# Operand tiles moved to multiples of 512 bytes in a gMLP and SSD trunk

## The chip, the cores and the metric

The kernel runs on one core of one Trainium2 chip. The metric is device time in microseconds of one execution; the time before is 1432.25 us, the median of three runs (1432.12 to 1435.49). The engines are TensorE (PE in the profile; its weight loads are PEld), VectorE (DVE), ScalarE (ACT), GpSimd (POOL) and SyncE (SP), which issues the loads. ScalarE's queue issues the stores.

## The reference

One layer on a sequence of 1024 positions with D = 1024. A normalised and modulated input h is projected to 11,296 columns, which feed two branches: a chunked spatial gating unit (gMLP) and a chunked state-space scan (SSD, 32 heads of 64, 8 groups). Both are projected back, gated, added, projected by w_out and added to the input; a last normalisation follows.

```python
mod = jax.nn.silu(c) @ ada_w + ada_b
shift, scale, gate = jnp.split(mod, 3, axis=-1)
h = rms_norm(x, norm_w) * (1 + scale[:, None, :]) + shift[:, None, :]
proj = h @ w_in
gm_u, gm_v, gm_z, ssm_z, xbc, dt_raw, g_a, g_b = jnp.split(proj, SPLITS, axis=-1)
y_a = spatial_gating(gelu(gm_u), gelu(gm_v), ...) * silu(gm_z)
xbc = silu(causal_depthwise_conv(xbc, conv_w, conv_b))
xs, bm, cm = jnp.split(xbc, ...)
dt = softplus(dt_raw + dt_bias)
a = -jnp.exp(a_log)
y_b = ssd_scan(xs as heads, dt, a, bm, cm) + xs * d_skip[:, None]
y_b = rms_norm(y_b * silu(ssm_z) by group)
merged = sigmoid(g_a) * (y_a @ w_proj_a) + sigmoid(g_b) * (y_b @ w_proj_b)
out = rms_norm(x + gate[:, None, :] * (merged @ w_out), final_norm_w)
```

## The kernel before

Nearly all matmuls of the projections work on float32r operands of 128 rows, with a stationary tile of 128 columns and a moving tile of 512. Each float32 operand is split into a high part (rounded to float32r) and the rest, and a product of two operands is three matmuls per block of 128: high with high, high with low, low with high. The small products of the state-space part are plain float32.

The work runs in five stages.

- The first stage (pool `p0`, to about 74 us) loads x and the modulation weights, computes h transposed, and writes it as the moving operands `bop` (names b11, t1, t2, b22, t3, b21, t4, each high and low, four tiles of 128 × 512). They stay in the pool `hp`, and after the products are done the same slots hold other operands. `first_products` makes the first 256 columns and dt beside it.
- The products (L563, `product`; to about 926 us) go over 43 pairs of 128-column blocks of w_in. A pair is done in a Winograd-like form with seven products of twelve matmuls. The weights of the pair after next are loaded to `wsp` (names a and s) and split into `wp` (names p..h and p..l). Each product ends with `run_tasks`, which runs small jobs that `later` put down for a number of products ahead: dt, the mixing weights, the gate, w_proj_b. The results go to the wide tiles `w4` and from there to DRAM.
- The state-space stage (to about 1176 us) runs chunks for eight groups (`Group`), with the projection by w_proj_a (`pma`) filled in between.
- The merge by w_proj_b (L1437, `multiply`; to about 1336 us) has 56 units of twelve matmuls. Its stationary tiles (p1a to p4a) lie in the pools `p2r` and `p2q`, its moving tiles (bh, bl) in `hp`.
- The output product (`out_product`, tiles po) multiplies merged rows (stationary mh and ml in `hp`, mmh and mml in `p2r` and `p2q`) with gated w_out (moving, woh and wol in `hp`).

Memory is laid out by pools. On the left a pool begins where the one opened before it ends: four small constants that the framework puts behind a scratch area of 16 KB, then `const`, `hp`, and then by turns `p0`, `wp` and `wsp`. On the right pools grow down from the top: `w4`, then `gm` and `gx` (later `prepool`), and after the products `p2r`, `p2x` and `p2q`. Within a pool tiles lie one behind the other, padded to 32 bytes. A pool that is opened with `reuse_waits="tile"` makes each of its tiles wait for the earlier tiles that it overlaps. The `const` pool holds 7,936 bytes per partition, among them `dtb`, `abc` and `dsk` of 128 bytes each (L112, L113, L115). At the narrowest, when `p2q` is open, left and right are 96 bytes apart (139,136 and 139,232).

The three small constants are used so: `dsk` is loaded in the first stage (L437) and two copies take it to `dskt` in `small_parameters` (L417). `dtb` and `abc` are loaded at the same place (L435, L436) and read in `dt_part1a` (L653) and `dt_part1d` (L680 to L682), some 670 us later.

The builder's planner sets the order of what isn't pinned (`pin` keeps program order) by its own estimate of times; TensorE's matmuls and the loads are pinned.

Of the kernel before, what the change touches and what calls it, by code (L numbers as in the profile page):

```python
# [8 lines left out]
F32 = mybir.dt.float32  # L9
# [7 lines left out]
P = 128  # L17
# [6 lines left out]
NH = 32  # L24
# [11 lines left out]
def hybrid_kernel(  # L36
# [33 lines left out]
    def cst(shape, name, dt=F32):  # L70
        return const.tile(shape, dt, name=name, tag=name)
# [9 lines left out]
    def f32(t):  # L81
        return t.bitcast(F32)

    def load(dst, src):
        pin(nc.sync.dma_start(dst, src))
# [23 lines left out]
    par = cst([P, P], "par")  # L109
    par2 = cst([P, P], "par2")  # L110
    cwt = cst([P, P], "cwt")
    dtb = cst([P, NH], "dtb")  # L112
    abc = cst([P, NH], "abc")  # L113
    dskt = cst([P, 16], "dskt")
    dsk = cst([P, NH], "dsk")  # L115
    sc = cst([P, KT], "sc")
    dthq = cst([P, NCH * NH], "dthq")
    dde = cst([P, NCH * NH], "dde")
# [30 lines left out]
    def last_split(nm):  # L149
# [2 lines left out]
        pin(A.copy(hi, t))  # L152
        pin(V.tensor_sub(lo, t, f32(hi)))

    w4pool = tc.tile_pool(name="w4pool", bufs=1, side="right", reuse_waits="tile")
    w4p = w4pool.__enter__()
    w4 = [w4p, 6]

    def wide(name, dt=F32):
        return w4[0].tile([P, S], dt, name=name, tag="w4", bufs=w4[1])  # L160


    with tc.tile_pool(name="p0", bufs=1, reuse_waits="tile") as p0:
# [8 lines left out]
        def aw_tile(n):  # L172
            return p0.tile([P, KT, 2, P], F32, name=f"aw{n}", tag="aw", bufs=2)

        hf2 = {}

        def hf_tile(k, h):
# [18 lines left out]
        def load_aw(n):  # L196
            k = KS[n]
            if n:
                aw[n] = aw_tile(n)
            for j in range(2):  # L200
                load(aw[n][:, :, j, :],
                     ada_w[:, j * D + k * P : j * D + (k + 1) * P].rearrange("(k p) c -> p k c", p=P))

        def load_w0(n):
            k = KS[n]
            raw = p0.tile([P, W0], F32, name=f"w0r{n}", tag="w0r", bufs=2)
            wd = p0.tile([P, 2 * NH], F32R, name=f"w0d{n}", tag="w0d", bufs=2)
            hi, lo = (p0.tile([P, 256], F32R, name=f"w0{v}{n}", tag=f"w0{v}", bufs=2) for v in "hl")
            load(raw, w_in[k * P : (k + 1) * P, COL_DT : COL_DT + W0])
            wk[n] = (raw, wd, hi, lo)  # L210

        def split_w0(n):
            raw, wd, hi, lo = wk[n]
            pin(A.copy(hi, raw[:, NH:W0]))
            pin(A.copy(wd[:, 0:NH], raw[:, 0:NH]))
            pin(V.tensor_sub(lo, raw[:, NH:W0], f32(hi)))
            pin(V.tensor_sub(wd[:, NH:], raw[:, 0:NH], f32(wd[:, 0:NH])))
# [119 lines left out]
        def first_products(n):  # L337
            raw, wd, wh, wl = wk[n]
            for h in halves(n):
                hh, hl = hhs[n, h]  # L340
                for m, (lw, r) in enumerate(((wh, hh), (wl, hh), (wh, hl))):
                    for i in (1, 2):
                        mm(accs[i][h], lw[:, i * P - P : i * P], r, n + m == 0, n == KT - 1 and m == 2)
                        yield
                for nd, r in ((2 * NH, hh), (NH, hl))[:: 1 if n == 0 else -1]:
                    mm(accs[0][h][0:nd, :], wd[:, 0:nd], r, n == 0 and r is hh, n == KT - 1 and r is hh)
                    yield
# [46 lines left out]
        def prepare(n):  # L394

            if n == 1:
                return {
                    8: lambda: (warm(6), transposes(0, 1), rows_of_h(0, 1), matvec(1), warm(5)),
                    11: lambda: (transposes(1, 1), modulation(1), rows_of_h(1, 1)),
                    16: lambda: (transposes(1, 0), rows_of_h(1, 0)),  # L400
                }
            a, b = halves(n)
            return {
                2: lambda: (matvec(n), transposes(n, a)),
                6: lambda: (modulation(n), rows_of_h(n, a)),
                14: lambda: (transposes(n, b), rows_of_h(n, b)),
            }

        def small_parameters():
            pp = ax("pp1")  # L410
            for i in range(2):
                tp(pp[:, i * P : (i + 1) * P], pkb[:, i], ident)
            for i in range(2):
                pin(V.tensor_copy((par2, cwt)[i], pp[:, i * P : (i + 1) * P]))
            for hh in range(2):
                part = slice(hh * HD, (hh + 1) * HD)
                pin(V.tensor_copy(dskt[part, :], dsk.rearrange("p (i h) -> p i h", h=2)[part, :, hh]))  # L417
# [10 lines left out]
        for n in range(KT):  # L428
            todo = prepare(n + 1) if n + 1 < KT else {}
            for at, _ in enumerate(first_products(n), 1):  # L430
                if at == 1 and n + 2 < KT:
                    load_aw(n + 2)
                    load_w0(n + 2)
                if at == 1 and n == 1:
                    load(dtb, dt_bias.to_broadcast([P, NH]))  # L435
                    load(abc, a_log.to_broadcast([P, NH]))  # L436
                    load(dsk, d_skip.to_broadcast([P, NH]))  # L437
                if at in todo:
                    todo[at]()
                for f, kk in sums.get((n, at), ()):  # L440
                    f(kk)
                if at == 2 and 0 < n < KT - 1:
                    split_w0(n + 1)
                if n == 4 and at == 8:
                    small_parameters()
# [7 lines left out]
    gm = gmpool.__enter__()  # L453
# [27 lines left out]
    def later(delay, f, *a):  # L481
        tasks.append((slot[0] + delay, f, a))
# [143 lines left out]


    bsb = gm.tile([P, D], F32, name="bsb", tag="bsb")
    first_c1 = {"v0": gx.tile([P, S], F32, name="c1v0", tag="wst")}
    wst = None  # L630
    bst = gx.tile([P, NCH, NG, 6], F32, name="bst", tag="bst")
# [3 lines left out]
    def dt_part1():  # L635

        dtt = wide("dtt2")[0 : 2 * NH, :]
        load(dtt, dt_d)
        V.tensor_add(fold[0], ident[:, 0:NH], ident[:, NH : 2 * NH])
        sm1 = wide("sm1").rearrange("p (a n) -> p a n", a=4)  # L640
        sm2 = wide("sm2").rearrange("p (a n) -> p a n", a=4)
        later(2, dt_part1a, dtt, sm1, sm2)
# [476 lines left out]
    def stats():  # L1119
        v_stats()  # L1120
        mix_load(0)

    later(216, dt_part1)
    later(9, mix_weights)
    for i in range(4):
# [554 lines left out]
```

## Time and profile before

| | before |
|---|---|
| median of three runs | 1432.25 us |
| profiled execution, span | 1432.7 us |
| PE busy | 1396.2 us, 97% |
| PEld busy | 1152.6 us, 80% |
| VectorE busy | 1024.9 us, 72% |
| ScalarE busy | 785.1 us, 55% |
| GpSimd busy | 205.7 us, 14% |
| mean clock of TensorE | 0.997 |
| DMA moved | 277.08 MB, 193 GB/s |

The profile is one execution. A matmul's duration there (some 390 ns) is modelled and overlaps with the next one's, so busy TensorE isn't TensorE at its best. How fast matmuls follow each other is read from their starts: in the timeline, or in the chain of waits, where a merged row "2.72 PE zx L563 x12" stands for twelve matmuls, one behind the other. The trace lacks some matmul records, so counts are taken from the code where they matter. An instruction's shape stands behind its name (128*128 128x512: array rows and columns used, then the moving tile).

### The profile page before, as it was taken

To read this page: it belongs to the slowest core of one execution; us is meant where nothing else is said; L and a number is where in the kernel's file an instruction comes from. 1 tells how busy PE (TensorE), PEld (TensorE's weight loads), DVE (VectorE), ACT (ScalarE), POOL (GpSimd) and SP (SyncE) were. 2 spreads that over 40 slices of the span, in tenths; PEclk is the share of its full clock that TensorE was granted. 3 is DMA by queue.
4 is the path that set the end of the run, shared out by engine and by line. 5 is a ranking of instruction groups with operands and counts; after the bars stand their busy time and mean duration, and the time that the engine had idled before them with its cause. 6 is when DMAs were issued, how large, how long until landed. Compare 5 with 4: busy or idle time off the path is not lost.

```text
span 1432.7 us, 20518 instructions
## 1 busy us (share of the span) xinstructions
PE 1396.2 (97%) x7087; PEld 1152.6 (80%) x7087; DVE 1024.9 (72%) x1821; ACT 785.1 (55%) x1444; POOL 205.7 (14%) x190
## 2 busy tenths in 40 slices
PE   8999999999999999999999999999989989999997
PEld 6688888888888888888887888877878877787886
DVE  5686776777667888788887784587677767948443
ACT  6664576566656565555665555776667524325101
POOL 0000000000000000000000100057878830000000
PEclk9999999999999999999999999999999999999999
DMA  8552343333332777687677764788778668977332
GB/s 266 162 162 89 118 118 103 107 100 118 103 114 86 205 223 225 190 246 215 195 231 216 220 180 142 268 297 307 254 262 295 215 211 286 352 254 284 124 118 74
DMA packets 260524, 277.08 MB, mean 193 GB/s; under 512 B 13596, under 2 KB 210628, under 8 KB 260420
## 3 DMA queue, kind: packets, MB, share of 16 engines
q1 hardware_dynamic: 179396, 195.37, 43.8%
q10 hardware_dynamic: 81024, 80.40, 16.6%
q8 instruction: 56, 0.92, 0.3%
q14 instruction: 48, 0.39, 0.1%
HBM read 191.40 MB, written 84.31 MB: 192 GB/s over the span
## 4 chain that ended last, share of the span: by engine, by line
PE 78%; DMA 8%; DVE 5%; issue 3%; ACT 3%; POOL 2%; SPq 1%; ACTq 0%; POOLq 0%; DVEq 0%
PE xuz L563 6%; PE po L76 6%; PE xcb L563 6%; PE xx L563 5%; PE xz L563 5%; PE x L1437 5%; PE xg L563 5%; PE pma L76 3%; PE yp L1437 3%; PE yuz L563 3%; PE xv L563 3%; PE ycb L563 3%; PE yx L563 3%; PE yz L563 2%; PE yg L563 2%
## 5 line engine op out<-in xcount | busy, mean ns | idle before, releaser
L770 POOL TENSOR_TENSOR wog<-wog,gb 128x1024 f32<-128x1024 f32 x8 | 21.8, 2722 | 724.8 <-PE xz L563 529.1
L969 ACT ACTIVATE dcy<-dcy,nacs 128x128 f32<-128x128 f32 x256 | 78.5, 389 | 14.4 <-POOL dcy L964 14.2
L964 POOL TENSOR_SCALAR_AFFINE_SELECT dcy<-dcy 128x1024 f32<-128x1024 f32 x32 | 35.1, 1097 | 107.8 <-ACT ea L961 104.1
L961 ACT ACTIVATE ea<-dcy 64x512 f32<-64x512 f32 x64 | 40.1, 627 | 12.6 <-DMA dcy<-acs_d 12.2
L882 ACT ACTIVATE ac<-ac 128x1024 f32<-128x1024 f32 x32 | 34.0, 1061 | 20.0 <-DVE ac L880 19.8
L1643 ACT ACTIVATE xr<-r 128x1024 f32<-128x1024 f32 x7 | 7.4, 1061 | 67.2 <-issue 39.7
L76 PE MATMUL pma<-yh,wah 128*128 128x512 f32 x128 | 43.9, 424 | 0.0
L76 PE MATMUL pma<-yh,wal 128*128 128x512 f32 x128 | 43.2, 419 | 0.0
L1049 DVE TENSOR_TENSOR ym<-yn,ea 128x512 f32<-128x512 f32 (+1 forms) x32 | 19.9, 623 | 31.3 <-PE yn L76 31.2
L1051 POOL TENSOR_TENSOR yz<-y,sl 128x512 f32<-128x512 f32 x32 | 41.9, 1309 | 1.1
L989 DVE TENSOR_TENSOR dcy<-dcy,pc 128x1024 f32<-128x1024 f32 x32 | 39.0, 1217 | 4.3 <-PE pc L79 3.0
L76 PE MATMUL pma<-yl,wah 128*128 128x512 f32 x128 | 40.5, 398 | 0.0
L76 PEld LDWEIGHTS yn<-sl,st 128*128 128x128 f32 x224 | 30.3, 190 | 10.9 <-POOL yz L1051 2.9
L1050 POOL TENSOR_TENSOR y<-y,ym 128x512 f32<-128x512 f32 (+1 forms) x32 | 36.5, 1142 | 16.3 <-DVE ym L1049 16.3
L1633 POOL TENSOR_TENSOR r<-r,fnw 128x256 f32<-128x256 f32 (+1 forms) x3 | 2.7, 916 | 250.7 <-ACT xr L1632 250.7
L76 PE MATMUL yn<-sl,st 128*128 128x128 f32 x224 | 31.7, 276 | 7.1 <-DVE st L1019 7.1
L880 DVE SCALAR_TENSOR_TENSOR ac<-c2x,cwt,ac 128x1023 f32<-128x1023 f32 (+2 forms) x24 | 31.8, 1325 | 9.0 <-ACT ac L878 7.1
L1642 DVE TENSOR_TENSOR r<-po,xr 128x1024 f32<-128x1024 f32 x7 | 8.6, 1225 | 41.1 <-PE po L76 41.1
L76 PE MATMUL sp<-xe,bn 128*128 128x256 f32 x112 | 33.0, 411 | 4.5 <-DVE ym L1049 1.4
L76 PE MATMUL yi<-dcy,xd 128*64 128x128 f32 x512 | 35.9, 284 | 0.0
L880 DVE SCALAR_TENSOR_TENSOR ac<-c2cb,cwt,ac 128x1023 f32<-128x1023 f32 (+2 forms) x24 | 30.6, 1275 | 7.1 <-ACT ac L878 7.0
L1017 POOL TENSOR_TENSOR st<-st,cd 128x256 f32<-128x256 f32 x48 | 32.3, 673 | 10.3 <-PE yn L76 7.2
(2827 smaller groups left out, 4395.4 us busy)
## 6 DMA issues: line engine op xcount, KB each, us to landing
sl<-s_d SPq DMA_DIRECT2D x32, 768.0 KB
s_d<-ac ACTq DMA_DIRECT2D x32, 512.0 KB
dcy<-acs_d SPq DMA_DIRECT2D x32, 512.0 KB
aw<-in_ada_w_dram SPq DMA_DIRECT2D x16, 512.0 KB
wbr<-in_w_proj_b_dram SPq DMA_DIRECT2D x64, 128.0 KB
wb_d<-wbb ACTq DMA_DIRECT2D x32, 256.0 KB
wb_d<-wbc ACTq DMA_DIRECT2D x32, 256.0 KB
yb_d<-yz ACTq DMA_DIRECT2D x32, 256.0 KB
```

Source lines behind the costliest of these rows:

```text
L76: pin(PE.matmul(acc, l, r, start=first, stop=last))
L563: pin(PE.matmul(ps, lw[:, k * P : (k + 1) * P], r[k], start=first and n + k == 0, stop=n == 2 and k == 3, skip_group_check=not first))
L880: V.scalar_tensor_tensor(ac[:, s:], cc[:, : S - s], conv_wt[:, 3 - s, i : i + 1], ac[:, s:], op0=ALU.mult, op1=ALU.add)
L882: A.activation(ac, ac, AF.Silu)
L961: A.activation(ea[hh * HD : (hh + 1) * HD], dcy.rearrange("p (j e) i l -> p e j (i l)", e=2)[hh * HD : (hh + 1) * HD, hh], AF.Exp)
L964: G.affine_select(out=d8, in_=d8, compare_op=ALU.is_ge, fill=-1e30, base=0, pattern=[[0, 2 * HPG], [1, P]], channel_multiplier=-1)
L969: A.activation(dcy[:, h, i, :], dcy[:, h, i, :], AF.Exp, bias=sub[:, i, h : h + 1])
L989: V.tensor_tensor(d3, d3, pc[:, 0:256].unsqueeze(1).to_broadcast([P, HPG, 256]), op=ALU.mult)
L1017: G.tensor_mul(v3(s2), v3(self.st), fac(cd, g, s)[:, i].unsqueeze(2).to_broadcast([P, HPG, HD]))
L1050: G.tensor_add(y1[:, :, t0:], y1[:, :, t0:], m[:, :, t0:])
L1051: G.tensor_mul(yz, y1, sl[:, 4:6])
L1437: pin(PE.matmul(ps[j], a[:, v, js], r, start=first and n + k == 0, stop=n == 2 and k == KT - 1, skip_group_check=not first))
```

## The change

Three things are done to the layout. `dtb`, `abc` and `dsk` leave the pool `const`; `dsk` becomes a tile of `p0`, and `dtb` and `abc` become the first and second 32 columns of a tile `dta` in `gm`. Their loads: `dsk`'s stays; those of the other two move to `dt_part1`, behind the reload of dt. And a pool `edge` with one tile of 120 floats (480 bytes) that nothing uses is opened first on the right.

The left pools behind `const` so move down by 384 bytes, from 24,448 to 24,064 = 47 × 512, and the top of the right pools by 480, from 229,344 to 228,864 = 447 × 512. The left and the right pools then meet at 138,752 when `p2q` is open. The tiles of `p0` behind x lie 128 bytes further along than a multiple would have them, as `dsk` stands before them. No instruction of TensorE, VectorE, ScalarE or GpSimd is added or removed.

```diff
-    dtb = cst([P, NH], "dtb")
-    abc = cst([P, NH], "abc")
     dskt = cst([P, 16], "dskt")
-    dsk = cst([P, NH], "dsk")
...
+    edge = ctx.enter_context(tc.tile_pool(name="edge", bufs=1, side="right"))
+    edge.tile([P, 120], F32, name="edge", tag="edge")
     w4pool = tc.tile_pool(name="w4pool", bufs=1, side="right", reuse_waits="tile")
...
+        dsk = p0.tile([P, NH], F32, name="dsk", tag="dsk")
...
                 if at == 1 and n == 1:
-                    load(dtb, dt_bias.to_broadcast([P, NH]))
-                    load(abc, a_log.to_broadcast([P, NH]))
                     load(dsk, d_skip.to_broadcast([P, NH]))
...
     bsb = gm.tile([P, D], F32, name="bsb", tag="bsb")
+    dta = gm.tile([P, P], F32, name="dta", tag="dta")
+    dtb, abc = dta[:, 0:NH], dta[:, NH : 2 * NH]
...
         load(dtt, dt_d)
+        load(dtb, dt_bias.to_broadcast([P, NH]))
+        load(abc, a_log.to_broadcast([P, NH]))
```

## The prediction

> **What bounds the kernel now.** I read the page first (busy times, clock, chain), then the stages in the view of stretches, then the chain in order of time, and then single matmuls in the timeline of TensorE.
>
> ```profile
> span 1432.7 us, 20518 instructions
> PE 1396.2 (97%) x7087; PEld 1152.6 (80%) x7087; DVE 1024.9 (72%) x1821; ACT 785.1 (55%) x1444; POOL 205.7 (14%) x190
> PEclk9999999999999999999999999999999999999999
> PE 78%; DMA 8%; DVE 5%; issue 3%; ACT 3%; POOL 2%; SPq 1%; ACTq 0%; POOLq 0%; DVEq 0%
> ```
>
> ```profile
> 0.00:74.00 74.00, 66.29 (x470) 49.35 (x471) 42.72 (x106) 48.24 (x90) 3.13 (x10) 1.00 0.70 207
> 74.00:616.00 542.00, 541.63 (x2486) 449.98 (x2485) 413.22 (x687) 327.39 (x521) 1.40 (x1) 1.00 0.47 140
> 616.00:926.00 310.00, 308.79 (x1369) 253.44 (x1368) 230.16 (x413) 178.87 (x310) 23.97 (x10) 1.00 0.68 207
> 926.00:1176.00 250.00, 231.83 (x1686) 200.16 (x1685) 182.96 (x328) 158.23 (x400) 174.41 (x166) 0.99 0.78 267
> 1176.00:1336.00 160.00, 158.86 (x678) 126.66 (x677) 117.71 (x189) 58.53 (x100) 0.00 (x0) 1.00 0.81 281
> 1336.00:1422.00 86.00, 86.00 (x386) 70.42 (x385) 34.58 (x90) 12.09 (x22) 1.28 (x1) 1.00 0.30 104
> ```
>
> In the second fence the columns are stretch, length, busy time (instructions) of PE, PEld, DVE, ACT and POOL, clock, DMA share, GB/s. TensorE is busy nearly everywhere, at full clock, and carries 78% of the chain. So what counts is how long one matmul takes, not whether TensorE waits. The chain gives that: almost pure TensorE from 78 to 616 us, products of 12 matmuls in 2.72 us.
>
> ```profile
> 212.28 2.72 PE zx L563 x12
> ...
> 853.21 3.02 PE xx L563 x12
> ```
>
> That is 226.7 ns for each matmul of 512 columns. Later products take up to 3.02 us, and DMAs and VectorE enter the chain there. Is 226.7 ns the array's own time? This stretch of the state-space stage has the clock at 0.50 (eighth number), and two matmuls stand there in 0.85 us:
>
> ```profile
> 1170.60:1173.28 2.68, 2.68 (x7) 2.11 (x8) 2.52 (x5) 1.76 (x3) 2.10 (x1) 0.50 0.93 316
> ...
> 1171.58 1.05 PE L76 MATMUL pma<-yl,wah 128*128 128x512 f32 x2
> 1172.43 1.05 PE L76 MATMUL pma<-yh,wal 128*128 128x512 f32 x2
> ```
>
> So 512 columns take 425 ns at half clock, 212.5 ns if all of it scaled to full clock. The product's matmul pays 14 ns more at full clock, for something that does not get faster with the array. A plain float32 matmul of 256 columns, which passes each column twice and so asks for its moving operand at half the rate, does not pay it:
>
> ```profile
> 933.25 0.81 PE L76 MATMUL sp<-xe,bn 128*128 128x256 f32 x3
> ...
> 933.68 0.38 PE L76 MATMUL sp<-xe,bn 128*128 128x256 f32 x1
> ```
>
> Between the first and the third start lie 0.81 − 0.38 = 0.43 us, 215 to 216 ns for 512 array steps. Hence the excess is in fetching operands, not in the array or in the handover between matmuls.
>
> Does the address matter? Tile sizes of the kernel before, added up (four built-in constants of 32 bytes, then 7,936 bytes of constants), start every tile of the left pools 384 bytes past a multiple of 512. The right pools grow down from 32 bytes below such a multiple, so theirs start at 480. The output stage mixes both: the moving operand is always on the left (wo), the stationary one on the left (mh, ml) or the right (mmh, mml), with the same line and shape.
>
> ```profile
> 1414.09 0.39 PE L76 MATMUL po<-woh,mh 128*128 128x512 f32 x1
> ...
> 1416.13 0.39 PE L76 MATMUL po<-woh,mmh 128*128 128x512 f32 x1
> ...
> 1418.23 0.40 PE L76 MATMUL po<-woh,mmh 128*128 128x512 f32 x1
> ```
>
> From 1414.09 to 1416.13 nine matmuls with left weights take 226.7 ns each; from 1416.13 to 1418.23 nine with right weights take 233.3 ns. The merge by w_proj_b (L1437) has its weights on the right too:
>
> ```profile
> 1298.96 0.64 PE L1437 MATMUL x<-p7bh,p7a 128*128 128x512 f32 x2
> ...
> 1302.48 0.63 PE L1437 MATMUL x<-p7bh,p7a 128*128 128x512 f32 x2
> ...
> 1173.87 0.62 PE L76 MATMUL pma<-yl,wah 128*128 128x512 f32 x2
> ...
> 1175.71 0.62 PE L76 MATMUL pma<-yh,wal 128*128 128x512 f32 x2
> ```
>
> Fifteen L1437 matmuls start between the first two rows, 234.7 ns each; the projection pma, both operands left but broken up by other work, takes 1.84/8 = 230 ns. So the start of an operand within 512 bytes is worth at least 7 to 8 ns of a matmul in this trace.
>
> [...]
>
> **The change, part by part.**
>
> *Addresses.* Without dtb, abc and dsk (128 bytes each) the left pools start at a multiple of 512, and the edge of 480 bytes puts the right pools on one. No row shows a matmul so aligned. Its bounds are 212.5 ns (half-clock row, scaled) and 234.7 ns (slowest row). I take 216 ns, the float32 rows: 384 bytes past a multiple leaves 128 bytes, 32 elements, in the first 512, and the 14 ns that a product pays are 34 columns at 212.5/512 = 0.415 ns each. That fits a fetch in blocks aligned to more than 128 bytes, whose partial first block costs time. It is a fit, not a proof.
>
> - Products, 43 pairs × 7 × 12 = 3612 matmuls (L563), 10.7 ns less: 38.6 us. By length 542/852 of them, 2298, lie in the pure-TensorE stretch up to 616 us: 24.6 us, counted whole, since VectorE, next there, is busy 413 of 542 us. The other 14.1 us lie where the chain already passes through DMAs and VectorE (230 of 310 us busy, DMA 0.68): half, 7.0.
> - pma, 8×8×3×2 = 384, 14 ns less: 5.4 us, in a stage where TensorE idles 18 us and GpSimd is busy 174 of 250: half, 2.7.
> - L1437, 56 × 12 = 672, 18.7 ns less: 12.6 us. DMA is at 0.81 and 281 GB/s there and would have to rise to 0.88 in the shorter stage: half, 6.3.
> - Output, 360 matmuls of 512 columns. 15 of its 32 operand tiles come from the right: 191 × 10.7 + 169 × 18 = 5.1 us, whole, since nothing else is near its limit.
> - First products, 128 × 10.7 = 1.4 us, in a stage where TensorE idles 8 us: 0.4.
>
> *Three constants.* The loads of dt_bias and a_log leave the first stage and are issued behind the reload of dt:
>
> ```profile
> 29.37 0.42 SPq L85 DMA_DIRECT2D dtb<-in_dt_bias_dram  x1
> 29.85 0.42 SPq L85 DMA_DIRECT2D abc<-in_a_log_dram  x1
> ...
> 673.31 0.50 SPq L85 DMA_DIRECT2D dtt<-dt_d  x1
> 675.07 0.37 SPq L85 DMA_DIRECT2D a11g<-in_w_in_dram  x1
> ...
> 697.01 0.42 DVE L653 TENSOR_TENSOR sm<-pdtt,dtb 128x256 f32<-128x256 f32 x1
> ```
>
> First read at 697.01 us, 23 us after the new place; SP idles 1.26 us behind dtt, which covers the two issues of 0.42. Price 0, without that cover 0.9 us; the gain early is at most 0.9 us and I take 0, since SP waits for buffers soon after. dsk keeps its load at the same place and is read by the same copies: 0.
>
> *Overlaps in time.* Later pools reuse the space of earlier ones and wait for the tiles they overlap. p2q now starts where wpool did (before, 96 bytes further in), so its 4 KB tiles cover two old slots instead of three. That can only remove waits; their price is at most the 18 us that TensorE idles in the state-space stage, and I take 0. In the first stage dsk shifts the aw tiles 128 bytes against the weight slots that follow them; both end with the same products, 0, at worst one product's 2.72 us.
>
> Sum: 24.6 + 7.0 + 2.7 + 6.3 + 5.1 + 0.4 = 46.1 us. 1432.7 − 46.1 = 1386.6; the median of the runs shown is 1432.25, 0.45 below the profiled span, so 1386.
>
> **Rivals.**
>
> *Only the difference of the two starts counts* (0.22). Then 0 and 0 is what 384 and 384 is, products stay at 226.7, and only right-hand weights gain: 672 × 8.0 = 5.4, half to all, and 169 × 6.6 = 1.1, so 4 to 6.5 us: 1427. For it: the rows above differ in just this. Against it: the 10.7 ns that float32 does not pay remain unexplained.
>
> *Alignment does nothing* (0.09): each read goes at its own rate wherever it starts, and the time stays at 1432. The 233.3 would have to come from something else that the right-hand tiles share, such as which pool filled them; nothing in the rows names it. [...]
>
> *Both reads starting on the same boundary collide* (0.12). The next weights load while a matmul streams (PEld 80% beside PE 97%); if both reads then meet in the same block, each matmul goes to the 234.7 ns of the slowest rows: 3612 × 8.0 = 28.9, pma 384 × 4.7 = 1.8, output 191 × 8 = 1.5, together +32: 1464. For it: nothing excludes that equal offsets are the worst at 0. Against it: equal offsets at 384 are the fastest seen. It decides as soon as an aligned matmul takes more than 228.3 ns, today's mean over all 5028 (3803 at 226.7, 384 at 230, 841 at 234.7).
>
> *As forecast, with more or less cover* (0.57): with all of it off the chain, 24.6 + 14.1 + 5.4 + 12.6 + 5.1 + 1.4 = 63.2 us, 1369; with 212.5 ns in addition 3.5 × 5028 = 17.6 less, 1351; with an aligned matmul at 222 ns, about half the gain, 1409. Its own range is 1360, midway between 1351 and 1369, to 1409.
>
> **How the numbers follow.** Runs of this kernel spread by 0.2%, so 0.3%, 4.3 us, is about what a measurement can tell from no change. Faster: 0.57 and nearly all of 0.22, 0.78. Same: 0.09 and the weakest of the second case, 0.10. Slower: 0.12. The range runs from 1360 to 1433, no change; it leaves out the collision and the last few us below.
>
> **What would show it.** Right: products of the chain at 12 × 216 ns = 2.59 us and the same step for left and right weights in the output stage. Second rival: products at 2.72, L1437 and the output at 226.7 throughout. Collision: products at 2.8 or more. A gain that does not arrive would show as idle time of TensorE between 616 and 926 and in 1176 to 1336, ended by DMA or VectorE. The dt part would be wrong if VectorE's L653 waited for a DMA.

## The result, and the profile after

The kernel with the new layout takes 1428.93 us (median of five runs, 1426.53 to 1430.96); the kernel before, run beside it on the same chip, 1434.69 us. The ratio is 0.9966, 95% interval 0.9953 to 0.9979: 3 to 7 us less. The forecast was 1386. The profiled execution took 1430.04 us, its span is 1428.3 against 1432.7 before. The two spans differ by 4.4 us, and that is the difference the rows below divide up.

First the page of the changed kernel:

```profile
span 1428.3 us, 20518 instructions
PE 1392.6 (97%) x7087; PEld 1153.7 (81%) x7087; DVE 1023.6 (72%) x1821; ACT 787.8 (55%) x1444; POOL 208.5 (15%) x190
PE 76%; DMA 9%; DVE 5%; issue 3%; ACT 3%; POOL 2%; SPq 1%; ACTq 0%; POOLq 0%; DVEq 0%
```

TensorE is busy 3.6 us less. The same stretches as in the prediction (length, then busy time and instructions of PE, PEld, DVE, ACT, POOL, clock, DMA share, GB/s) show where:

```profile
74.00:616.00 542.00, 541.62 (x2484) 449.87 (x2483) 413.79 (x687) 328.50 (x520) 1.25 (x1) 1.00 0.46 140
616.00:926.00 310.00, 308.62 (x1365) 252.93 (x1365) 228.95 (x412) 178.90 (x308) 26.02 (x10) 1.00 0.67 206
1176.00:1336.00 160.00, 157.58 (x692) 128.93 (x691) 120.63 (x194) 60.02 (x102) 0.00 (x0) 1.00 0.80 285
```

In the stretch 74 to 616 us TensorE gets through 2484 matmuls, before 2486: the products run at the old pace. In 1176 to 1336 it gets through 692, before 678. The chain (start, length, matmuls) gives the time of one. A product of twelve, then the merge by w_proj_b and the output:

```profile
104.15 2.72 PE yv L561 x12
...
1222.71 43.13 PE yp L1439 x189
...
1290.93 41.89 PE x L1439 x183
1332.82 84.78 PE po L76 x384
```

The same three rows of the kernel before:

```profile
1222.86 44.54 PE yp L1437 x189
...
1292.77 43.14 PE x L1437 x183
1335.91 86.05 PE po L76 x384
```

A product stands at 2.72 us, 226.7 ns a matmul, to the digit as before. 189 matmuls of the merge went from 44.54 to 43.13 us, 7.5 ns each, and the output stage from 86.05 to 84.78 us. Left and right weights of the output stage are now alike. The timeline has four runs of three matmuls between the first and the second row (left weights, mh and ml) and four between the second and the third (right weights, mmh and mml), 2.72 us both times:

```profile
1409.11 0.39 PE L76 MATMUL po<-woh,mh 128*128 128x512 f32 x1
...
1411.83 0.39 PE L76 MATMUL po<-woh,mmh 128*128 128x512 f32 x1
...
1414.55 0.28 PE L76 MATMUL po<-woh,mh 128*128 128x256 f32 x1
```

From its first to its last matmul the merge takes 156.0 us instead of 159.3, the output stage 87.75 instead of 89.0: 4.6 us together, against 4.4 in the spans. That is the rival "only the difference of the two starts counts", with its own signs (products at 2.72, the rest at 226.7) and its own size (4 to 6.5 us). It left open why the matmuls stay at 226.7 ns.

### The profile page after: what moved, and what is told of

The parts are those of the page before. It is cut to its first block, busy times and chain, and to the rows that moved or that the text cites. A ratio compares the mean times of both kernels' runs of the same rounds, so it can differ in the third digit from the quotient of the medians.

```text
span 1428.3 us, 20518 instructions
## 1 busy us (share of the span) xinstructions
PE 1392.6 (97%) x7087; PEld 1153.7 (81%) x7087; DVE 1023.6 (72%) x1821; ACT 787.8 (55%) x1444; POOL 208.5 (15%) x190
## 4 chain that ended last, share of the span: by engine, by line
PE 76%; DMA 9%; DVE 5%; issue 3%; ACT 3%; POOL 2%; SPq 1%; ACTq 0%; POOLq 0%; DVEq 0%
PE xuz L561 6%; PE po L76 6%; PE xcb L561 6%; PE xx L561 6%; PE x L1439 5%; PE xz L561 5%; PE xg L561 4%; PE yuz L561 3%; PE yp L1439 3%; PE pma L76 3%; PE xv L561 3%; PE ycb L561 3%; PE yx L561 3%; DMA dcy<-acs_d 3%; PE yz L561 2%
```

## The experiments

**The edge alone, and the constants alone.** The first kernel is the one before with nothing but an edge of 96 bytes on the right, so that right and left pools both begin 384 bytes past a multiple of 512. The second is the changed one without its edge, so the left begins on a multiple and the right 480 past one.

```diff
 # before, plus
+    edge = ctx.enter_context(tc.tile_pool(name="edge", bufs=1, side="right"))
+    edge.tile([P, 24], F32, name="edge", tag="edge")
```

> The kernel before with an unused edge of 96 bytes on the right and nothing else: left and right tiles both start 384 bytes past a multiple of 512, no constant is moved. Theory 'difference': the merge by w_proj_b and the output product go at 226.7 ns as in the changed kernel, 1427 to 1430 us, the same as it. Theory 'multiple of 512': no gain, 1432 to 1435.

> The changed kernel without its edge: the three constants moved, left tiles at multiples of 512, right tiles at 480. Theory 'difference': stationary 32 bytes short of the moving one's start, so the gain of the merge and of the output product is gone or changed (each matmul 227 to 238 ns), 1431 to 1437 us. Theory that moving the constants and loads makes the gain: 1427 to 1430, as the changed kernel.

Measured: 1427.6 us with the edge alone, ratio to before 0.9959 (0.9945 to 0.9972), and 1434.38 us with the constants alone, ratio 0.9999 (0.9988 to 1.0011). Chain rows of the edge alone, then of the constants alone:

```profile
103.24 2.72 PE yv L565 x12
...
1225.24 43.13 PE yp L1439 x189
```

```profile
104.21 2.72 PE yv L559 x12
...
1223.78 44.37 PE yp L1437 x189
```

The merge gains wherever both sides start alike, at 384 and 384 as much as at 0 and 0, and no product gains anywhere. Moving the constants, their loads and the changed overlaps of the pools are worth nothing measurable: the terms taken as 0 were 0 within the 1.6 us that this interval leaves.

**One matmul, by the start of its operands.** A kernel of rows of 30 equal matmuls, with nothing to wait for; it leaves out the rest of the computation.

```diff
+    for i in range(30):
+        pin(PE.matmul(acc, B[:, s // 4 : s // 4 + 128], B[:, m // 4 : m // 4 + 512], start=i == 0, stop=i == 29))
```

> A kernel of matmuls alone, which leaves out the whole computation: 74 rows of 30 float32r matmuls (128 x 512 moving, 128 stationary columns) that differ in where the two operands start. The moving operand stands at 0 and the stationary one at 0 to 496 in steps of 16 bytes; then both at the same start from 32 to 480; then stationary 96 bytes behind moving at four places; then narrower operands, bfloat16 and plain float32. Theory 'difference' (only the distance between the two starts within 512 bytes counts): equal starts 226.7 ns everywhere, 96 bytes apart 234 to 235 everywhere, other distances somewhere between 216 and 238, and the same at every place. Theory 'block' (the start itself counts, as in the prediction): equal starts differ from place to place. If some distance gives under 226.7, a layout with that distance beats both kernels, at 216 by about 45 us. bfloat16, with half the bytes, should stand at 216.

Its timeline, cut at the beginning of a row of 30 (each answer begins with the last matmul of the row before). Between consecutive lines here lie 30 matmuls with the weights 0, then 96, then 256 bytes off the moving operand:

```profile
26.33 7.19 PE L75 MATMUL acc<-B 128*128 128x512 f32 x31
33.13 7.19 PE L75 MATMUL acc<-B 128*128 128x512 f32 x31
...
74.67 7.43 PE L75 MATMUL acc<-B 128*128 128x512 f32 x31
81.71 7.39 PE L75 MATMUL acc<-B 128*128 128x512 f32 x31
...
144.27 7.19 PE L75 MATMUL acc<-B 128*128 128x512 f32 x31
151.07 7.20 PE L75 MATMUL acc<-B 128*128 128x512 f32 x31
```

6.80, 7.04 and 6.80 us, so 226.7, 234.7 and 226.7 ns. The means from the starts in the second half of each row:

```
float32r 128x512, moving operand at a multiple of 512, weights d bytes past one
d     0      16     32     64     96     128    160    176    192    208    224    240    256    272
ns    226.7  226.7  233.5  233.2  234.5  233.7  233.3  230.3  228.9  233.3  233.2  226.7  226.7  226.7
beyond 256 the same row repeats; both at 32, 64 ... 480: 226.7 throughout;
96 apart with the moving operand at 0, 128, 256, 384: 234.1 to 234.3
columns   float32r: 512 226.7, 384 173.3, 256 120.0    bfloat16: 512 215.8, 256 109.2
plain float32, by record (each matmul has two): 512 429.2, 256 215.8
```

Two neighbouring bfloat16 rows, the first of 512 columns with the operands 96 bytes apart (6.48 us, 216 ns), the second of 256 columns:

```profile
484.02 6.86 PE L75 MATMUL acc<-H 128*128 128x512 bf16 x31
490.50 3.65 PE L75 MATMUL acc<-H 128*128 128x512 bf16 x31
```

Four things follow, for the starts and widths tried. Only the distance counts, not the place (both at 32 to 480: 226.7 ns; 96 apart at four places: 234.1 to 234.3). It counts modulo 256 bytes, not 512 (226.7 ns at 0 and at 256). No distance gets below 226.7 ns. And 128 columns cost 53.3 ns (173.3 − 120.0), with 13.3 ns on top of each float32r matmul whether it has 512, 384 or 256 columns (120.0 − 106.7), some 2.5 on top of each bfloat16 one (109.2 − 106.7). The 13.3 ns are there at every start tried, so they are no partial first block.

**The modulus, in the kernel.** The changed kernel with other edges: 224 bytes (right pools 256 past a multiple of 512, left at 0) and 352 bytes (right 128 past).

```diff
-    edge.tile([P, 120], F32, name="edge", tag="edge")
+    edge.tile([P, 56], F32, name="edge", tag="edge")
```

> After, with an edge of 224 bytes in place of 480: left pools begin at a multiple of 512, right pools 256 bytes past one. If the difference of the two starts counts modulo 256, as in the row of matmuls by offset, this is as good as after: 1427 to 1431 us, L1439 and both weights of the output stage at 226.7 ns. If multiples of 512 count, it is as before: 1433 to 1437 us with the right-hand weights at 233 ns.

> After, with an edge of 352 bytes: left pools at a multiple of 512, right pools 128 bytes past one. By the difference modulo 256 right-hand weights take 233.7 ns as before, and the time is 1433 to 1437 us. If it is enough that every tile begins at a multiple of 128 bytes, 1427 to 1431 us.

Measured: 1429.12 us, ratio to before 0.9971 (0.9957 to 0.9985), and 1433.29 us, 0.999 (0.9974 to 1.0007). The rows of the merge, 224 first:

```profile
1222.06 43.17 PE yp L1439 x189
```

```profile
1220.31 44.19 PE yp L1439 x189
```

At 256 apart as fast as at 0, at 128 apart nearly as slow as at 96 (44.54): modulo 256 holds in the kernel too, and multiples of 512 are not needed.

**The products' weights moved 128 bytes away.** The changed kernel without its edge, and 128 unused bytes at the end of `hp`. That puts the weights of the products 128 bytes off their moving operands, 0 before; the merge and the output are left as they were.

```diff
+    hp.tile([P, 32], F32, name="gap", tag="gap")
...
-    edge = ctx.enter_context(tc.tile_pool(name="edge", bufs=1, side="right"))
-    edge.tile([P, 120], F32, name="edge", tag="edge")
```

> After without the edge, and with 128 unused bytes at the end of hp, so that the weights of the products (wp) stand 128 bytes off their moving operands (hp); everything else is as in the kernel without the edge. By the difference of starts the products go from 226.7 to 233.7 ns, 2.80 us for twelve, and 3612 x 7.0 = 25 us are added to 1434: 1459 us if the whole of it arrives, 1452 if half of the 14 us outside pure TensorE time is hidden. If the start of the products' weights means nothing for them, 1434 us.

```profile
span 1444.5 us, 20520 instructions
PE 1415.1 (98%) x7087; PEld 1156.8 (80%) x7087; DVE 1027.3 (71%) x1821; ACT 788.8 (55%) x1444; POOL 205.7 (14%) x190
```

```profile
103.34 2.78 PE yv L560 x12
106.12 2.79 PE zv L560 x12
...
1189.80 13.99 PE x L1438 x60
```

A product takes 2.78 to 2.79 us where it took 2.72, 5.4 ns a matmul where 7.0 were expected; why less than in the rows of equal matmuls stays open. From the first to the last matmul of the products the stage is 17.5 us longer than without the gap (870.2 against 852.7 us), the merge begins 13 us later (1189.80, against 1176.65 in the row below), and the run takes 1450.81 us, ratio to before 1.0107 (1.0084 to 1.0131), some 15 us. The two kernels' spans differ by 11.5. So the direction is as expected, the matmul's part was put too high, and not all of it reaches the end.

```profile
1176.65 13.99 PE x L1437 x60
```

This is the kernel without edge and gap; these 60 matmuls of the merge take the same to the digit in both.

**Where the 10.7 ns come from.** A second kernel of matmul rows varies one operand at a time.

```diff
+    st = B[:, s // 4 : s // 4 + 1].to_broadcast([P, 128])   # weights: one column again and again
+    mv = B[:, m // 4 : m // 4 + 1].to_broadcast([P, 512])   # moving: one column again and again
```

> Leaves out the whole computation: rows of 30 matmuls (128x128 by 128x512, one PSUM bank) without waits, one operand varied at a time. It asks where the 10.7 ns come from that a float32r matmul costs above the 216 ns of a bfloat16 one, and whether any arrangement of the operands avoids them. Theory A, a fixed cost of each float32r matmul: 226.7 ns stays whatever the strides, the rows used (64 or 32 instead of 128) or the widths alternated (512 with 256 gives the mean of 226.7 and 120.0, 173.3), and float32r alternating with bfloat16 gives the mean, 221.3. Theory B, the weights' read is the cost: weights read from one repeated column (stride 0) or from 64 rows give 216, moving data from one repeated column still 226.7. Theory C, the moving read is the cost: the other way round, moving data from one repeated column give 216, and a stride of two elements in it costs much more. Starts 4 to 28 bytes apart: as 0 if the read goes by blocks of 32 bytes or more (226.7), else 233.5 from the first element on.

The timeline again, two neighbouring rows each for a moving operand of every second column (first pair), weights of one repeated column (second) and a moving operand of one repeated column (third):

```profile
236.20 14.24 PE L103 MATMUL acc<-B 128*128 128x512 f32 x31
249.80 14.26 PE L103 MATMUL acc<-B 128*128 128x512 f32 x31
...
338.63 7.34 PE L103 MATMUL acc<-B 128*128 128x512 f32 x31
345.58 7.34 PE L103 MATMUL acc<-B 128*128 128x512 f32 x31
...
359.10 6.94 PE L103 MATMUL acc<-B 128*128 128x512 f32 x31
365.66 6.94 PE L103 MATMUL acc<-B 128*128 128x512 f32 x31
```

13.60, 6.95 and 6.56 us for 30: 453, 231.7 and 218.7 ns. With a single weight column read again and again, a matmul takes some 232 ns whether the operands start at the same place or 96 bytes apart (full operands: 226.7 and 234.3). With a single moving column it takes 218.7 ns in both cases: 8.0 of the 10.7 ns are gone, and with them the cost of the distance. A moving operand with a stride of two doubles the time (453.3 is 2 × 226.7), weights with a stride of two or four columns take 230 to 240 ns, and 64 operand rows at equal starts still take 226.7. So theory B falls, and theory A too, though alternating widths of 512 and 256 give the mean, 173 ns, as it had said (512 and 384 give 207 where 200 were due). Theory C comes nearest: most of the 10.7 ns hang on the moving operand's read. Its 216 ns were not reached, a stride was not tried in bfloat16, and why the 13.3 ns are the same at 512, 384 and 256 columns these rows don't show. Starts 4 to 12 bytes apart give 231 to 233 ns, 16 apart 226.7, 244 and 252 apart 226.7, but 248 apart 233.3: the law within 16 bytes stays open. Float32r alternating with bfloat16 takes 460 ns a pair where 442.5 were due. The rows with 64 operand rows 96 bytes off and with 32 ran at about half clock (PEclk 5 and 5, in tenths, in the page's slices from 386 to 407 us) and say nothing.

**A version without that read.** If a 4-byte moving operand costs 10.7 ns, the two cross terms of a product can be read as bfloat16, since a low part and its partner need few bits.

```diff
-        for n, (lw, r) in enumerate(((lh, rh), (lh, rl), (ll, rh))):
+        for n, (lw, r) in enumerate(((lh, rh), (ll[:, 512:1024], rl), (ll[:, 0:512], r16))):
...
-                keep(V.tensor_sub(lo, t, f32(hi)))
+                keep(V.tensor_sub(lo[:, 0:512], t, f32(hi)))
+                keep(A.copy(lo[:, 512:1024], t))
```

> After, with the two cross terms of every product of the first two stages (low with high, high with low) computed from bfloat16 operands; high with high stays float32r. The low parts are written as bfloat16 straight away, and a bfloat16 copy of each high part is added: 301 copies of 128x512 for the weights, on ScalarE, some 36 for the moving operands, most on GpSimd. If it is the read of a float32r moving operand that costs 226.7 ns in place of 215.8 ns, a product takes 4 x 226.7 + 8 x 215.8 = 2.63 us in place of 2.72, 301 products 26 us less: 1403 us if all of it arrives, 1408 if half of what lies behind 616 us is hidden. If changing between the two types costs as much as the row of alternating matmuls showed (pairs of 460 ns where 442 were due, 9 ns a change), two changes a product take 5 us of it back: 1408 to 1413. If ScalarE, 0.59 us a copy and 178 us more in 852, becomes the bound, no gain or a loss: 1429 or more.

> The same, with the 301 copies for the weights on GpSimd, which is idle in the stage of the products to 616 us. By the read of the moving operand: 1403 to 1408 us as on ScalarE, if a copy takes GpSimd less than the 2.6 us of a product and does not slow VectorE; if it slows VectorE or comes late, TensorE waits at the products (idle time before L561 ended by POOL) and the time is above that of the kernel with the copies on ScalarE.

Measured: 1442.27 us with the copies on ScalarE, ratio to before 1.0054 (1.0031 to 1.0077), and 1448.84 us with them on GpSimd, 1.0101 (1.0079 to 1.0124). Yet the products did get faster. The timeline of the first, and its waits of TensorE between 497 and 937 us (total, times, longest):

```profile
200.30 1.90 PE L583 MATMUL zuz<-b21l,p2uz0l 128*128 128x512 bf16 x8
201.85 1.28 PE L583 MATMUL xuz<-t3h,p7uz0h 128*128 128x512 f32 x4
202.97 1.90 PE L583 MATMUL xuz<-t3l,p7uz0l 128*128 128x512 bf16 x8
```

```profile
PE xg L583 <- DVE c2g L599: 5.7, 3, 4.3
PE xx L583 <- DVE c2x L599: 2.7, 2, 1.8
PE ycb L583 <- ACT p5cb L599: 2.0, 1, 2.0
...
```

The same view of the changed kernel has three rows:

```profile
PE xz L561 <- DVE c2z L577: 0.6, 1, 0.6
PE xg L561 <- DVE c2g L577: 0.4, 1, 0.4
PE xx L561 <- DVE c2x L577: 0.4, 1, 0.4
```

From 200.30 to 202.97 us lies one product, 2.67 us: 0.05 less than 2.72, where 0.09 were due without the changes of type. Over 301 products that is 15 us. More than that is lost again. The first stage ends 8 us later (products from 83.1 us instead of 75.1), and further on TensorE waits 13 us for sums, 1.4 in the changed kernel. The state-space stage, which this edit leaves alone, also takes 252.7 us from the last product to the merge instead of 247.4; why was not followed. Together this explains some 10 of the 12.1 us between the two spans. ScalarE is at 926 us instead of 788. On GpSimd the same copies bring VectorE from 1024 to 1105 us busy, and it is slower still. Two more divisions of the copies were tried:

```diff
-            pin(G.tensor_copy(h16, hf))
+            pin(V.tensor_copy(h16, hf))
...
 # the second of the two, besides
-                keep(A.copy(lo[:, 512:1024], t))
+                keep(G.tensor_copy(lo[:, 512:1024], t) if nm in ("p3", "p7") else A.copy(lo[:, 512:1024], t))
```

> The kernel with bfloat16 cross terms and ScalarE's copies, but with the copies of the first stage on VectorE (moving operands) and ScalarE (weights) instead of GpSimd, which was busy 35 us there and with which the products began at 83 us and not at 75. If GpSimd was what delayed that stage, 6 to 8 us come back: 1434 to 1437 us. If it was the added copies as such (28 on VectorE's 44 us of 74), no more than 2 us: 1440 to 1443.

> The same, and two of seven copies of the weights (p3 and p7) on GpSimd, which takes 51 us off ScalarE. TensorE waited 13 us between 497 and 937 us for sums that follow ScalarE's work, 1.4 us in the kernel after. If ScalarE's load is the cause, about half of that comes back, and with the products at 2.67 us (0.05 less than 2.72, 15 us over 301) the time is 1425 to 1432; if any added copy delays it, 1434 to 1443.

Measured: 1441.32 us, 1.0053 (1.0027 to 1.008), and 1433.8 us, 0.9997 (0.9977 to 1.0018). In both the products begin at 81 us, so GpSimd's work is at most 2 of the 8 us by which the first stage is late; that the added copies as such are the rest is by elimination. Taking two of seven copies off ScalarE brings 7.5 us, which fits its load being part of the cost later on. TensorE's waits between 485 and 937 us only fall from 12.7 to 10.6 us in the two profiled executions, so this is not shown; 1433.8 lies between the two ranges given. None of the four beats 1428.93; what delays the first stage in them was not followed further.

## Why the prediction was wrong

It took the right view first: TensorE bounds the kernel, and the length of one matmul decides. That 1428.93 us lies within the range of 1360 to 1433 speaks for none of its mechanism: the range reached up to no change, and what happened is the rival "only the difference of the two starts counts". Point by point:

- *"I take 216 ns": the step that failed.* The difference between 226.7 and 216 ns was put down to a partial first block of the moving operand, because 14 ns are about the 32 elements that lie before the next multiple of 512 bytes at a start of 384. The prediction called that a fit. In the rows of matmuls the 13.3 ns stand at every start and every width tried, so aligned operands keep 226.7 ns, and no run shows a float32r matmul of 512 columns at 216. Most of the 10.7 ns hang on the read of the float32r moving operand: one repeated column takes 8.0 of them away. How that read makes the cost is open. The plain float32 row, quoted as proof that the array can do 216, was no like case: one record of it takes 256 columns in 215.8 ns, where float32r takes them in 120.0, so it asks for its operand at about half the rate (106.7 ns per 128 columns against 53.3); bfloat16 (215.8 ns for 512) has half the bytes. The trace shows two records for each plain float32 matmul (112 for the 56 of sp in the code); that one record is 512 array steps was the author's estimate from its time, and no run counts steps.
- *Products, 38.6 us, 31.6 of them counted:* 0 (2.72 us before and after). *pma, 2.7:* both operands lie left before and after, so their distance did not change. *First products, 0.4:* no gain seen; they begin and end as before within 0.7 us. Here the distance did change, and not for the better: `dsk` puts the tiles of `p0` behind it 128 bytes off the moving operands in `hp`.
- *L1437, 18.7 ns × 672, 6.3 us:* 7.5 ns in place of 18.7, read on 189 of them; 672 × 7.5 = 5.0 us, of which 3.3 arrive in the stage. TensorE's waits there for sums that VectorE makes (p, L1555, and c, L1549) went from 1.1 to 1.9 us, and a pause of 0.5 us for issue is new: with these 1.3 us it is 4.6 of 5.0. No wait for a DMA, the cover that the prediction named, appeared there. That the waits for DVE came from the shorter matmuls isn't shown either: the kernel with the constants alone, whose merge gains next to nothing, has 1.4 us of the same waits and 0.3 us for issue.
- *Output, 5.1 us:* 1.3. Its part for right-hand weights, 169 × 6.6 = 1.1 us in the rival, arrives whole, as the prediction said of that stage.
- *Constants, 0, and overlaps, 0:* right, by the kernel with the constants alone (0.9999). No wait for a DMA appeared at L653 (L655 in the changed kernel).
- *"Only the difference of the two starts counts", 0.22:* this is what happened, with its terms, 4 to 6.5 us. The objection to it (the 10.7 ns stay unexplained) did not bear on it. A second effect without an explanation doesn't count against the explanation of the first.
- *"Both reads starting on the same boundary collide":* the other way round. Equal starts are the fastest, at 0 as at 384 (226.7 ns in the rows of matmuls).
- *The halves and wholes by cover* could not be tested by a gain that was not there. The gap shows them from the other side: 5.4 ns on 3612 matmuls are 19.5 us; 17.5 are in the stage and some 15 in the time, about three quarters, where the prediction counted 31.6 of 38.6, about four fifths.

## What to carry to other kernels

If one operand of many float32r matmuls lies left and the other right, bring the starts of the two pools to the same place modulo 256 bytes: 96 unused bytes gave all of this change's gain, 7 ns on each matmul concerned, and the place itself doesn't matter. Where operands already stand equally, alignment brings nothing, and 226.7 ns for 512 columns is the least that any layout tried here reached in float32r. Before a residue of a few nanoseconds times 5000 is forecast to vanish, look for a row in which it does vanish under the same conditions; a plain float32 row, which takes its columns at about half the rate (256 of them in 215.8 ns, float32r in 120.0), is not the same condition.

## What the runs showed of the hardware

- A float32r matmul costs 13.3 ns beside its columns (53.3 ns per 128), at 512, 384 and 256 columns (226.7, 173.3 and 120.0 ns); a bfloat16 one some 2.5 ns, at 512 and 256 (215.8 and 109.2 ns). With one repeated moving column it falls from 226.7 to 218.7 ns, with a stride of two it rises to 453.3.
- Distances of moving operand and weights of 0, 16 and 240 bytes modulo 256 cost a float32r matmul nothing (226.7 ns); those between, in steps of 16, cost it 2 to 8 ns (228.9 to 234.5 ns). A bfloat16 one takes 215.8 ns at 0 and at 96 apart, the two distances tried. With one repeated moving column the float32r cost of the distance is gone (218.7 ns at 0 and at 96).
- A change between float32r and bfloat16 costs some 9 ns in a row of alternating matmuls (460 ns a pair, 442.5 due), and a product with two changes takes 0.04 us more than its matmuls add up to (2.67 us, 2.63 due); that the changes make this difference too isn't shown apart.
